# A transformer block on one core: DeltaNet's inverse doubling in eight steps, and a head's output transposes moved behind two later projections

## The chip, the cores and the metric

The kernel runs on one core of one Trainium2 chip. The metric is the device time of one execution in microseconds (us).

## What is computed

The program is one block of a diffusion transformer over 1024 tokens of width 1024 with a context of 256 tokens: layer norm and modulation, a wide input projection, a branch of differential attention (8 heads), a branch of gated DeltaNet (8 heads), a merge, and an MLP. All is in float32. The change lies in the DeltaNet branch alone. For each head and each of two directions (the sequence and its reverse) the reference computes this, chunk by chunk:

```python
a_mat = jnp.where(strict, jnp.einsum('bhnid,bhnjd->bhnij', kb, kc) * decay, 0.0)
t_mat = lax.linalg.triangular_solve(eye + a_mat, jnp.broadcast_to(eye, a_mat.shape),
                                    left_side=True, lower=True, unit_diagonal=True)
...
def step(state, xs):
    u_i, w_i, qk_i, q_i, k_i, g_i = xs
    v_new = u_i - jnp.einsum('bhid,bhde->bhie', w_i, state)
    o_i = jnp.einsum('bhid,bhde->bhie', q_i, state) + jnp.einsum('bhij,bhje->bhie', qk_i, v_new)
    state = state * g_i[..., None, None] + jnp.einsum('bhid,bhie->bhde', k_i, v_new)
    return state, o_i
...
return (rms_norm(o, norm_g) * jax.nn.silu(z)).reshape(b, length, DN_WIDTH)
```

q, k and v are projections that pass through a convolution of 7 taps and a silu; z is a projection too.

## The kernel before

The kernel works on chunks of 128 tokens: 10 chunks (2 of the context, 8 of the sequence) in each direction.

**Projections.** One head needs v, k, q and z of DeltaNet, and between them two projections ("f") of other parts of the block are filled in. `gemm_cols` (L157) computes one projection in two halves of 512 tokens, each 24 matmuls of 128x512: float32 is kept by splitting operands in a high and a low part, three matmuls for each of 8 blocks of the contraction (L167 to L169). The weights come over SP's DMA queue (L149), ScalarE makes the high part (L152), GpSimd the low part (L153). Two raw pieces and one whole projection's split pieces fit in the buffers. A projection's PSUM tile is called `pg`, of which there are two.

**A head's stages.** `dn_prep` transposes k and q, builds decay masks and, per chunk, the triangular matrix `cm` and the masked product `pm`, and inverts all diagonal 32x32 blocks on VectorE (`inverse32`, 46 operations on 104 partitions). The block inverses go to DRAM as `xd` and `yd`. `dn_double` (L587) loads them back as diagonal blocks into `cm` and `tt` (7 DMAs a direction, on SP), and builds the 128x128 inverse from 32x32 blocks by two doublings: products of 32x32, then of 64x64, with copies on VectorE (`z`, L615, L632) and ScalarE (L620, L625, L637) between. `tt` has one buffer, so direction 1's loads wait until direction 0's third product (L631) has read it. `dn_pre` makes token-major copies of v and k. `dn_chain` (L660) walks the 10 chunks of both directions: L683, L691, L679 on TensorE, ScalarE's `ws` (L686) and VectorE's `xs` (L681) and `S` (L696) depend on each other in a ring. At its end the head's output is normalized on VectorE (L722), transposed on TensorE (L726, 8 transposes into PSUM tile `po`), multiplied by the gate (L728) and written to DRAM as `odn_d` (L730).

**What sets the order.** Each engine runs one static list. A list scheduler makes it when the program is built: each operation has a rank, smaller first. The projections are written at a base rank of 6; the chain, the doubling within it and the weight loads have rank 0 (`R_CHAIN`, `R_W`), evictions of projections 0 (`R_E`), prep and pre 1 (`R_PREP`), convolutions 2 (`R_CONV`). In each turn h of the head loop the code writes pre(h), prep(h+1), double(h), chain(h), and then the projections `v`(h+1), `k`(h+2), `q`(h+2), f, f, `z`(h+1).

Of the kernel before, what the change touches and what calls it, by code (L numbers as in the profile page):

```python
# [8 lines left out]
F32 = mybir.dt.float32  # L9
# [47 lines left out]
class K:  # L57
    def __init__(self, tc, ins, out, ctx):
        self.tc, self.nc, self.i, self.out, self.ctx = tc, tc.nc, ins, out, ctx
        self.ranks = None  # L60
        self.weng = tc.nc.vector

# [94 lines left out]
    def gemm_cols(self, w, u, toks, evac, cs=slice(0, P), pool=None):  # L157
# [429 lines left out]
    def dn_double(self, h, r):  # L587
# [3 lines left out]
        tt = []  # L591
        for d in range(2):
            t = dw.tile([P, NT, 64], F32, name="tt", bufs=BK[0])
            for b, (lo, hi) in (((0, (32, 128)), (1, (64, 128)), (2, (96, 128))) if d else ((1, (0, 32)), (2, (0, 64)), (3, (0, 96)))):
                nc.gpsimd.memset(cm[d][32 * b:32 * b + 32, :, lo:hi], 0.0)
            nc.gpsimd.memset(t[96:128, :, 0:32] if d else t[0:32, :, 32:64], 0.0)
# [8 lines left out]
        for d in range(2):  # L605
            c_, t_ = cm[d], tt[d]
            pairs = ((3, 2), (1, 0)) if d else ((0, 1), (2, 3))
            sl = lambda b: slice(32 * b, 32 * b + 32)
            co = lambda b: slice(32 * (b % 2), 32 * (b % 2) + 32)
            pz = self.po.tile([P, NT, 32], F32, name="po")  # L610
            z = dw.tile([P, NT, 32], F32, name="z32", bufs=1)
            for a, b in pairs:
                for c in range(NT):
                    nc.tensor.matmul(pz[sl(b), c], lhsT=c_[sl(a), c, sl(b)], rhs=t_[sl(a), c, co(a)], start=True, stop=True)
                nc.vector.tensor_copy(out=z[sl(b)], in_=pz[sl(b)])  # L615
            py = self.po.tile([P, NT, 32], F32, name="po")
            a, b = pairs[0]
            for c in range(NT):
                nc.tensor.matmul(py[sl(b), c], lhsT=c_[sl(b), c, sl(b)], rhs=z[sl(b), c], start=True, stop=True)
            nc.scalar.copy(out=t_[sl(b), :, co(a)], in_=py[sl(b)])  # L620
            px = self.po.tile([P, NT, 32], F32, name="po")
            for a, b in pairs:
                for c in range(NT):
                    nc.tensor.matmul(px[sl(a), c], lhsT=z[sl(b), c], rhs=c_[sl(b), c, sl(b)], start=True, stop=True)
                nc.scalar.copy(out=c_[sl(a), :, sl(b)], in_=px[sl(a)])  # L625
            A, B = (slice(64, 128), slice(0, 64)) if d else (slice(0, 64), slice(64, 128))
            z6 = dw.tile([P, NT, 64], F32, name="z64", bufs=1)
            for q in range(2):
                pz = self.po.tile([P, 5, 64], F32, name="po")
                for c in range(5):  # L630
                    nc.tensor.matmul(pz[B, c], lhsT=c_[A, 5 * q + c, B], rhs=t_[A, 5 * q + c, :], start=True, stop=True)  # L631
                nc.vector.tensor_copy(out=z6[B, 5 * q:5 * q + 5], in_=pz[B])  # L632
            for q in range(2):
                px = self.po.tile([P, 5, 64], F32, name="po")
                for c in range(5):
                    nc.tensor.matmul(px[A, c], lhsT=z6[B, 5 * q + c], rhs=c_[B, 5 * q + c, B], start=True, stop=True)
                nc.scalar.copy(out=c_[A, 5 * q:5 * q + 5, B], in_=px[A])  # L637
# [22 lines left out]
    def dn_chain(self, h, r):  # L660
# [61 lines left out]
        nc.vector.tensor_tensor(out=oacc, in0=oacc, in1=so.unsqueeze(2).to_broadcast((P, NX, P)), op=ALU.mult)  # L722
        for q in range(2):
# [868 lines left out]
    def dn_phase(self):  # L1592
# [70 lines left out]
```

## Time and profile before

| | us |
|---|---|
| median of 3 runs | 3171.98 (3169.81 to 3173.66) |
| the profiled execution | 3170.53 |
| its span | 3168.8 |
| its mean granted TensorE clock | 0.949 |
| TensorE busy | 2899.6 (92%) |
| VectorE busy | 2263.7 (71%) |
| ScalarE busy | 1402.7 (44%) |
| GpSimd busy | 947.4 (30%) |

Busy time is a share of the whole span, in which stages with different limits follow one another. The DeltaNet phase lies between about 200 and 1290 us; the attention, merge and MLP behind it hold the rest. A start time below is counted from the span's start. A TensorE row's duration is the time to its modelled end, and matmuls overlap, so the distance between two starts tells what one costs.

### The profile page before, as it was taken

The numbers are of one execution on the slowest core, as the hardware profiler recorded it, in microseconds if no ns is written. First come the engines' busy times: TensorE is split into PE (matmuls) and PEld (weight loads), VectorE is DVE, ScalarE is ACT, GpSimd is POOL, SyncE is SP. The second block draws the span as 40 slices with busy tenths as digits, with TensorE's granted clock in tenths as the row PEclk, the third lists the DMA queues.
The fourth block names the chain that finished last, engine by engine and source line by source line (L and its number), as shares of the span: only waits on it lengthen the run. The fifth ranks groups of instructions, "written<-read, shape, count | busy, mean of one in ns | idle before, by whom it ended". The sixth has DMA issues, their size and how long they took to land. (4 is left out here: it accounts for less than half of the span.)

```text
span 3168.8 us, 45399 instructions
## 1 busy us (share of the span) xinstructions
PE 2899.6 (92%) x15736; PEld 2248.4 (71%) x15736; DVE 2263.7 (71%) x4202; ACT 1402.7 (44%) x3485; POOL 947.4 (30%) x959
## 2 busy tenths in 40 slices
PE   7998979989999899899999999999998999787888
PEld 4876767767778687677776777676776777566666
DVE  4678588777695873577777777644667775699999
ACT  4654344444344442355545555554456222233332
POOL 1235133342432421101000101111004533767771
PEclk9999889999998997999999999999999999898999
DMA  7531211221211212623222222316554543422222
GB/s 257 187 93 40 52 50 54 47 63 38 63 50 44 65 47 51 156 50 79 71 63 60 67 73 63 92 46 217 162 188 148 162 138 106 166 82 80 85 85 92
DMA packets 368118, 295.29 MB, mean 93 GB/s; under 512 B 88916, under 2 KB 321492, under 8 KB 366864
## 3 DMA queue, kind: packets, MB, share of 16 engines
q1 hardware_dynamic: 347920, 252.14, 27.1%
q10 hardware_dynamic: 16384, 29.54, 3.6%
q0 software_dynamic: 3584, 10.71, 0.9%
q8 instruction: 124, 2.03, 0.3%
q14 instruction: 106, 0.87, 0.1%
HBM read 212.08 MB, written 66.06 MB: 88 GB/s over the span
## 5 line engine op out<-in xcount | busy, mean ns | idle before, releaser
L153 POOL TENSOR_TENSOR wlo<-wraw,whi 128x256 fp32r<-128x256 f32 x312 | 316.6, 1020 | 1314.5 <-ACT whi L152 1146.5
L167 PE MATMUL pg<-uh,whi 128*128 128x512 f32 x1152 | 486.8, 423 | 9.4 <-ACT whi L152 6.1
L169 PE MATMUL pg<-uh,wlo 128*128 128x512 f32 x1152 | 485.3, 421 | 6.0 <-POOL wlo L153 5.9
L168 PE MATMUL pg<-ul,whi 128*128 128x512 f32 x1152 | 483.0, 419 | 0.0
L152 ACT CAST whi<-wraw 128x256 fp32r<-128x256 f32 (+1 forms) x568 | 240.9, 430 | 346.0 <-PE pg L168 95.2
L167 PEld LDWEIGHTS pg<-uh,whi 128*128 128x128 f32 x1152 | 225.7, 196 | 55.5 <-ACT whi L152 8.2
L169 PEld LDWEIGHTS pg<-uh,wlo 128*128 128x128 f32 x1152 | 225.1, 195 | 55.8 <-POOL wlo L153 11.2
L168 PEld LDWEIGHTS pg<-ul,whi 128*128 128x128 f32 x1152 | 225.2, 195 | 41.5 <-issue 4.1
L899 DVE TENSOR_REDUCE mp<-sx 128x1 f32<-128x1024 f32 x128 | 155.9, 1220 | 100.8 <-PE sx L889 100.5
L153 DVE TENSOR_TENSOR wlo<-wraw,whi 128x256 fp32r<-128x256 f32 (+1 forms) x256 | 135.4, 539 | 118.5 <-ACT whi L152 117.3
L985 PE MATMUL pa<-B,A 128*128 128x512 f32 x256 | 110.1, 431 | 69.7 <-DVE acc L1436 37.7
L1335 ACT CAST A<-araw 128x384 fp32r<-128x384 f32 (+1 forms) x144 | 66.7, 476 | 236.1 <-DVE araw L1344 107.3
L904 ACT ACTIVATE p<-sx,mx 128x1024 f32<-128x1024 f32 x128 | 143.4, 1121 | 43.4 <-DVE mx L900 39.1
L927 PEld LDWEIGHTS pat<-V,aT 128*128 128x128 f32 x1280 | 151.3, 194 | 13.2 <-ACT aT L925 10.9
L927 PE MATMUL pat<-V,aT 128*128 128x128 f32 x1280 | 159.8, 280 | 0.1
L925 ACT COPY aT<-pat 128x384 f32<-128x384 f32 (+1 forms) x192 | 78.3, 408 | 129.5 <-PE pat L924 121.3
L889 PE MATMUL sx<-kl,Q 64*128 64x512 f32 x256 | 128.3, 501 | 0.0
L924 PE MATMUL pat<-ident,p 128*128 128x128 f32 x640 | 118.8, 284 | 10.2 <-ACT aT L925 5.4
L1337 DVE TENSOR_TENSOR A<-araw,A 128x384 fp32r<-128x384 f32 (+1 forms) x144 | 123.6, 865 | 2.8 <-ACT A L1335 2.7
L888 PE MATMUL sx<-K,Q 128*128 128x512 f32 x256 | 118.9, 465 | 0.0
L985 PEld LDWEIGHTS pa<-B,A 128*128 128x128 f32 x256 | 52.0, 203 | 90.3 <-ACT A L1335 39.5
L924 PEld LDWEIGHTS pat<-ident,p 128*128 128x128 f32 x640 | 77.8, 142 | 53.6 <-ACT aT L925 19.0
(480 smaller groups left out, 7705.7 us busy)
## 6 DMA issues: line engine op xcount, KB each, us to landing
wraw<-in_w_in_dram SPq DMA_DIRECT2D x288, 128.0 KB
wraw<-in_w_in_dram SPq DMA_DIRECT2D x64, 256.0 KB
adraw<-in_w_ada_dram SPq DMA_DIRECT2D x128, 128.0 KB
uraw<-in_w_mlp_dram SPq DMA_DIRECT2D x32, 512.0 KB
braw<-in_w_mlp_dram SPq DMA_DIRECT2D x32, 512.0 KB
ff_d<-ue SPq DMA_DIRECT2D x52, 256.0 KB
araw<-ff_d SPq DMA_DIRECT2D x32, 384.0 KB
wa<-in_w_ada_dram SPq DMA_DIRECT2D x8, 1024.0 KB
```

The lines of the kernel that those rows point to most:

```text
L152: nc.scalar.copy(out=hi, in_=raw)
L153: self.weng.tensor_tensor(out=lo, in0=raw, in1=hi.bitcast(F32), op=ALU.subtract)
L167: nc.tensor.matmul(o, lhsT=hi, rhs=a, start=k == 0, stop=False)
L168: nc.tensor.matmul(o, lhsT=hi, rhs=b, start=False, stop=False)
L169: nc.tensor.matmul(o, lhsT=lo, rhs=a, start=False, stop=k == KT - 1)
L889: nc.tensor.matmul(ps, lhsT=q, rhs=low, start=False, stop=True)
L899: nc.vector.tensor_reduce(out=mp[:, m, 0:1], in_=px[m], axis=AX.X, op=ALU.max)
L904: nc.scalar.activation(out=p[:, CTX:], in_=px[m], func=AF.Exp, bias=mx[:, m:m + 1], accum_out=sp[:, 0, m:m + 1])
L924: nc.tensor.transpose(out=pt[:, c], in_=a[:, (c0 + c) * P:(c0 + c + 1) * P], identity=self.ident)
L927: nc.tensor.matmul(po, lhsT=aT[:, c], rhs=r["v"][:, c], start=c == 0, stop=c == NT - 1)
L985: nc.tensor.matmul(ps, lhsT=ah, rhs=bh, start=k == 0 and not add, stop=False, **more)
L1337: eng.tensor_tensor(out=z[1], in0=x, in1=z[0].bitcast(F32), op=ALU.subtract)
```

## The change

`dn_double` no longer issues its work. It returns eight closures, four for each direction: `first` (32x32 products, z), `second` (32x32 products into `tt` and `cm`), `third` (64x64 products, z) and `fourth` (64x64 products into `cm`). `gemm_cols` calls the next of them behind each half of a projection, as long as the list `between` holds any. The list for head h+1 is made ahead of `q`(h+2) in turn h, so that it is used up by q, f, f and z(h+1); what is left is called at the top of the next turn. For head 0, two empty closures stand ahead of the eight. The matmuls are now written at the projections' rank instead of the chain's, their copies and loads at `R_PREP`, and their PSUM tiles come from `pt` instead of `po`. Direction 0's loads are issued in its first step, direction 1's at the end of direction 0's third. The transposes of the output, the gate product and the DMA move to `dn_finish`, which is called behind the projections of v and k; for the last head, behind `fill(100)`.

```diff
@@ gemm_cols
             with self.rank(R_E):
                 evac(o, t0, n)
+            if self.between and pool is None:
+                self.between.pop(0)()
@@ dn_double
-        for d in range(2):
-            t = dw.tile([P, NT, 64], F32, name="tt", bufs=BK[0])
...
-            for b in range(4):
-                s = slice(32 * b, 32 * b + 32)
-                nc.sync.dma_start(out=cm[d][s, :, s], in_=(yd if d else xd)[d, b].rearrange("c j i -> j c i"))
-                if b != (0 if d else 3):
-                    o = 32 * (b % 2)
-                    nc.sync.dma_start(out=t[s, :, o:o + 32], in_=(xd if d else yd)[d, b].rearrange("c j i -> j c i"))
-            tt.append(t)
+        def load(d):
+            with self.rank(R_PREP):
+                t = tt[d] = dw.tile([P, NT, 64], F32, name="tt", bufs=BK[0])
...
+        def steps(d):
...
+            def first():
+                if d == 0:
+                    load(0)
+                t_, pz = tt[d], self.pt.tile([P, NT, 32], F32, name="pt")
+                z = zt[d] = dw.tile([P, NT, 32], F32, name="z32", bufs=1)
+                for a, b in pairs:
+                    for c in range(NT):
+                        nc.tensor.matmul(pz[sl(b), c], lhsT=c_[sl(a), c, sl(b)], rhs=t_[sl(a), c, co(a)], start=True, stop=True)
+                    with self.rank(R_PREP):
+                        nc.vector.tensor_copy(out=z[sl(b)], in_=pz[sl(b)])
...
+            def third():
...
+                    with self.rank(R_PREP):
+                        nc.vector.tensor_copy(out=z6[B, 5 * q:5 * q + 5], in_=pz[B])
+                if d == 0:
+                    load(1)
...
+            return [first, second, third, fourth]
+
+        return steps(0) + steps(1)
@@ dn_chain
+        r["o"] = oacc
+
+    def dn_finish(self, h, r):
+
+        nc = self.nc
+        oacc, sz = r["o"], r["z"]
         for q in range(2):
             pt = self.po.tile([P, 4, P], F32, name="po")
@@ the head loop
         proj(0, "v")
+        self.between = [lambda: None] * 2 + self.dn_double(0, R[0])
         proj(1, "k", "q")
         proj(0, "z")
         for h in range(H):
+            while self.between:
+                self.between.pop(0)()
...
             with self.rank(R_CHAIN):
-                self.dn_double(h, R[h])
                 self.dn_chain(h, R[h])
             if h == H - 1:
                 self.fill(100)
+                self.dn_finish(h, R[h])
                 self.fill_head()
-            for c in ORD:
+            for n, c in enumerate(ORD):
+                if n == 2:
+                    if h + 1 < H:
+                        self.dn_finish(h, R[h])
+                        self.between = self.dn_double(h + 1, R[h + 1])
```

The order on TensorE shows where the steps come to stand. Names are out<-in; `pg` is a projection, `tt`, `cm` and `z` are the doubling's, `pc` the chain's. This is the doubling of head 3's second direction before; it lies among the steps of the first direction's chain:

```order
L679 MATMUL pc_7569<-S_7545,kT 128x128
L531 MATMUL pt<-qT,kT 128x128 x2
L168 MATMUL pg<-ul,whi 128x512
L683 MATMUL pc_7569<-xs_7571,cm 128x128
L614 MATMUL po<-tt,cm 32x32 x10
L169 MATMUL pg<-uh,wlo 128x512
L167 MATMUL pg<-uh,whi 128x512
L168 MATMUL pg<-ul,whi 128x512
L614 MATMUL po<-tt,cm 32x32 x10
L619 MATMUL po<-z_7413,cm 32x32 x10
L169 MATMUL pg<-uh,wlo 128x512
```

The first direction had its doubling ahead of the chain, with projections between its groups. After the change the same head's doubling of both directions reads like this, from its second group on:

```order
L633 MATMUL pt<-z_6725,cm 32x32 x10
L170 MATMUL pg<-uh,wlo 128x512
L168 MATMUL pg<-uh,whi 128x512
L169 MATMUL pg<-ul,whi 128x512
L639 MATMUL pt<-cm,z_6725 32x32 x10
L170 MATMUL pg<-uh,wlo 128x512
L624 MATMUL pt<-tt,cm 32x32 x10
L649 MATMUL pt<-tt,cm 64x64 x10
L639 MATMUL pt<-cm,z_6725 32x32 x10
L660 MATMUL pt<-cm,z_6877 64x64 x10
L624 MATMUL pt<-tt,cm 32x32 x20
L633 MATMUL pt<-z_6999,cm 32x32 x10
```

The second direction (from the `x20`) follows the first at once, and nothing of the chain or of the projections stands between.

The second place is the start of head 3's chain on TensorE. Before:

```order
L683 MATMUL pc_7501<-vtok,cm 128x128
L470 MATMUL pt<-ugh,r_gt 128x512
L470 MATMUL pt<-ugl,r_gt 128x512
L473 MATMUL pt<-r_neg_130,r_id 128x512
L691 MATMUL pc_7501<-ws_7503,ktok 128x128
L169 MATMUL pg<-uh,wlo 128x512
L167 MATMUL pg<-uh,whi 128x512
L168 MATMUL pg<-ul,whi 128x512
L679 MATMUL pc_7515<-S_7506,kT 128x128
L169 MATMUL pg<-uh,wlo 128x512
```

After (L712, L720 and L708 are the chain's L683, L691 and L679; L678 and L685 belong to `dn_pre`, L492 to `dn_prep`):

```order
L712 MATMUL pc_7508<-vtok,cm 128x128
L678 MATMUL pt<-ident,vT 128x128 x3
L685 MATMUL pt<-ident,kT 128x128 x8
L720 MATMUL pc_7501<-ws_7503,ktok 128x128
L720 MATMUL pc_7508<-ws_7510,ktok 128x128
L685 MATMUL pt<-ident,kT 128x128 x2
L492 MATMUL pt<-ident,kT 128x128
L708 MATMUL pc_7515<-S_7506,kT 128x128
L492 MATMUL pt<-ident,kT 128x128
L708 MATMUL pc_7525<-S_7513,kT 128x128
```

Both directions now step together, and transposes of the same and the next head stand where matmuls of the projections stood. Of a head's 288 projection matmuls, 254 stand in one stretch behind the chain and prep, and `dn_finish`'s transposes stand behind the first 73 of these.

## Rows read from the trace of the kernel before

**Rows 1.** The page's head, and its busy time by engine.

```profile
span 3168.8 us, 45399 instructions
...
PE 2899.6 (92%) x15736; PEld 2248.4 (71%) x15736; DVE 2263.7 (71%) x4202; ACT 1402.7 (44%) x3485; POOL 947.4 (30%) x959
```

**Rows 2.** Busy time by stretch: length, engines' busy (count), granted clock, DMA share, GB/s.

```profile
443.25:573.60 130.35, 119.70 (x831) 95.89 (x830) 106.92 (x240) 66.97 (x191) 54.67 (x64) 0.96 0.20 53
682.30:834.20 151.90, 138.17 (x884) 111.30 (x884) 108.52 (x249) 69.05 (x195) 56.70 (x69) 0.90 0.20 54
1093.00:1204.30 111.30, 104.86 (x774) 86.07 (x774) 81.29 (x191) 47.80 (x128) 28.53 (x36) 0.98 0.21 55
1204.30:1289.40 85.10, 83.67 (x589) 67.25 (x589) 26.42 (x83) 27.86 (x85) 9.06 (x13) 0.78 0.17 44
```

**Rows 3.** TensorE's waits, 200 to 1350: us in total, times, longest.

```profile
PE po L726 <- DVE oacc L722: 25.9, 7, 10.9
...
PE po L614 <- DMA tt<-yd: 4.1, 2, 2.3
```

**Rows 4.** TensorE's timeline, pieces: start, duration, instruction, [idle before].

```profile
323.82 0.81 PE L614 MATMUL po<-tt,cm 32*32 32x32 f32 x20
...
1093.04 0.81 PE L614 MATMUL po<-tt,cm 32*32 32x32 f32 x20
...
1201.81 0.39 PE L168 MATMUL pg<-ul,whi 128*128 128x512 f32 x1
1202.04 0.40 PE L169 MATMUL pg<-uh,wlo 128*128 128x512 f32 x1
1204.27 0.79 PE L614 MATMUL po<-tt,cm 32*32 32x32 f32 x20 [1.83 <-DMA tt<-yd]
...
1206.77 1.27 PE L619 MATMUL po<-z,cm 32*32 32x32 f32 x20
...
1224.55 0.79 PE L683 MATMUL pc<-vtok,cm 128*128 128x128 f32 x2
...
1289.43 1.09 PE L726 MATMUL po<-ident,oacc 128*128 128x128 f32 x8 [1.30 <-DVE oacc L722]
```

**Rows 5.** Busy time by stretch, in two doublings, columns as in rows 2.

```profile
573.00:593.00 20.00, 20.00 (x218) 16.55 (x218) 10.94 (x29) 6.65 (x15) 8.21 (x13) 1.00 0.10 16
...
1205.00:1225.00 20.00, 20.00 (x145) 14.74 (x143) 1.97 (x4) 2.72 (x7) 1.82 (x3) 0.51 0.17 36
```

**Rows 6.** SP's queue, waits between 200 and 1300.

```profile
SPq L602 <- PE po L631: 101.1, 8, 15.1
```

**Rows 7.** VectorE's timeline, first operation and last copy of head 0's inverse.

```profile
274.70 0.47 DVE L568 TENSOR_TENSOR slY<-slX,slL 104x2 f32<-104x2 f32 x1
...
317.63 1.11 DVE L548 COPY slY<-slX 104x1024 f32<-104x1024 f32 x1
```

**Rows 8.** VectorE by line, 330 to 1200: busy us, mean ns | idle before.

```profile
L443 DVE SCALAR_TENSOR_TENSOR kT<-cvraw,taps,kT 128x772 f32<-128x772 f32 (+1 forms) x72 | 64.1, 891 | 0.0
L568 DVE TENSOR_TENSOR slY<-slX,slL 104x2 f32<-104x2 f32 (+14 forms) x105 | 52.1, 496 | 0.8
...
L585 DVE TENSOR_REDUCE slX<-slY 104x64 f32<-104x256 f32 (+3 forms) x28 | 22.8, 814 | 0.4
...
L632 DVE COPY z<-po 64x320 f32<-64x320 f32 x28 | 13.7, 489 | 44.8 <-PE po L631 44.7
```

**Rows 9.** ScalarE by line, 330 to 1200, columns as in rows 8.

```profile
L686 ACT ACTIVATE ws<-pc,bdl 128x128 f32<-128x128 f32 x126 | 46.2, 368 | 78.2 <-PE pc L683 76.8
...
L625 ACT COPY cm<-po 32x320 f32<-32x320 f32 x28 | 11.7, 416 | 37.1 <-PE po L624 37.1
```

**Rows 10.** TensorE's timeline in head 2's chain, one chain step apart.

```profile
614.27 0.39 PE L691 MATMUL pc<-ws,ktok 128*128 128x128 f32 x2
...
617.53 0.49 PE L691 MATMUL pc<-ws,ktok 128*128 128x128 f32 x2
```

More of the change, by code (lines that the diff above doesn't have):

```diff
@@ L61, in __init__ @@
         self.weng = tc.nc.vector
+        self.between = []
     def pool(self, name, bufs=1, **kw):
@@ L590, in dn_double @@
         cm, xd, yd = r["cm"], r["xd"], r["yd"]
-        tt = []
-        for d in range(2):
-            t = dw.tile([P, NT, 64], F32, name="tt", bufs=BK[0])
-            for b, (lo, hi) in (((0, (32, 128)), (1, (64, 128)), (2, (96, 128))) if d else ((1, (0, 32)), (2, (0, 64)), (3, (0, 96)))):
-                nc.gpsimd.memset(cm[d][32 * b:32 * b + 32, :, lo:hi], 0.0)
-            nc.gpsimd.memset(t[96:128, :, 0:32] if d else t[0:32, :, 32:64], 0.0)
-            for b in range(4):
-                s = slice(32 * b, 32 * b + 32)
-                nc.sync.dma_start(out=cm[d][s, :, s], in_=(yd if d else xd)[d, b].rearrange("c j i -> j c i"))
-                if b != (0 if d else 3):
-                    o = 32 * (b % 2)
-                    nc.sync.dma_start(out=t[s, :, o:o + 32], in_=(xd if d else yd)[d, b].rearrange("c j i -> j c i"))
-            tt.append(t)
@@ L605, in dn_double @@
-        for d in range(2):
-            c_, t_ = cm[d], tt[d]
-            pairs = ((3, 2), (1, 0)) if d else ((0, 1), (2, 3))
[L608 to L612, printed above, removed]
-                for c in range(NT):
[L614 to L637, printed above, removed]
@@ new lines, in dn_double @@
+        sl = lambda b: slice(32 * b, 32 * b + 32)
+        co = lambda b: slice(32 * (b % 2), 32 * (b % 2) + 32)
+        tt, zt = {}, {}
+        def load(d):
+            with self.rank(R_PREP):
+                t = tt[d] = dw.tile([P, NT, 64], F32, name="tt", bufs=BK[0])
+                for b, (lo, hi) in (((0, (32, 128)), (1, (64, 128)), (2, (96, 128))) if d else ((1, (0, 32)), (2, (0, 64)), (3, (0, 96)))):
+                    nc.gpsimd.memset(cm[d][32 * b:32 * b + 32, :, lo:hi], 0.0)
+                nc.gpsimd.memset(t[96:128, :, 0:32] if d else t[0:32, :, 32:64], 0.0)
+                for b in range(4):
+                    s = sl(b)
+                    nc.sync.dma_start(out=cm[d][s, :, s], in_=(yd if d else xd)[d, b].rearrange("c j i -> j c i"))
+                    if b != (0 if d else 3):
+                        o = 32 * (b % 2)
+                        nc.sync.dma_start(out=t[s, :, o:o + 32], in_=(xd if d else yd)[d, b].rearrange("c j i -> j c i"))
@@ new lines, in steps, with second, fourth @@
+        def steps(d):
+            c_ = cm[d]
+            pairs = ((3, 2), (1, 0)) if d else ((0, 1), (2, 3))
+            A, B = (slice(64, 128), slice(0, 64)) if d else (slice(0, 64), slice(64, 128))
+            def first():
[8 more added lines that the diff above has]
+                        nc.vector.tensor_copy(out=z[sl(b)], in_=pz[sl(b)])
+            def second():
+                t_, z = tt[d], zt[d]
+                py = self.pt.tile([P, NT, 32], F32, name="pt")
+                a, b = pairs[0]
+                for c in range(NT):
+                    nc.tensor.matmul(py[sl(b), c], lhsT=c_[sl(b), c, sl(b)], rhs=z[sl(b), c], start=True, stop=True)
+                with self.rank(R_PREP):
+                    nc.scalar.copy(out=t_[sl(b), :, co(a)], in_=py[sl(b)])
+                px = self.pt.tile([P, NT, 32], F32, name="pt")
+                for a, b in pairs:
+                    for c in range(NT):
+                        nc.tensor.matmul(px[sl(a), c], lhsT=z[sl(b), c], rhs=c_[sl(b), c, sl(b)], start=True, stop=True)
+                    with self.rank(R_PREP):
+                        nc.scalar.copy(out=c_[sl(a), :, sl(b)], in_=px[sl(a)])
+            def third():
+                t_ = tt[d]
+                z6 = zt[d] = dw.tile([P, NT, 64], F32, name="z64", bufs=1)
+                for q in range(2):
+                    pz = self.pt.tile([P, 5, 64], F32, name="pt")
+                    for c in range(5):
+                        nc.tensor.matmul(pz[B, c], lhsT=c_[A, 5 * q + c, B], rhs=t_[A, 5 * q + c, :], start=True, stop=True)
+                    with self.rank(R_PREP):
+                        nc.vector.tensor_copy(out=z6[B, 5 * q:5 * q + 5], in_=pz[B])
+                if d == 0:
+                    load(1)
+            def fourth():
+                z6 = zt[d]
+                for q in range(2):
+                    px = self.pt.tile([P, 5, 64], F32, name="pt")
+                    for c in range(5):
+                        nc.tensor.matmul(px[A, c], lhsT=z6[B, 5 * q + c], rhs=c_[B, 5 * q + c, B], start=True, stop=True)
+                    with self.rank(R_PREP):
+                        nc.scalar.copy(out=c_[A, 5 * q:5 * q + 5, B], in_=px[A])
+            return [first, second, third, fourth]
```

## The prediction

> **What bounds the kernel now.** The page comes first, for the whole: span 3168.8 us, TensorE busy 92% [rows 1]. The change touches only the DeltaNet phase, from about 320 to 1290 us, so the table by head comes next, one stretch from the start of one head's doubling to the start of the next head's [rows 2]. In it TensorE is busy for 91 to 94% of most stretches, and no other engine comes near: the period of a head is TensorE's work, plus what it idles, plus what the lower clock takes. The six periods from the first doubling at 323.82 to the seventh at 1093.04 last 769.2 us, 128.2 us each; the eighth doubling follows 111.2 us later, the last chain starts 20.3 us after that, and the last output transposes 64.9 us after that [rows 4]. The list of waits names what TensorE idles for: the biggest entry is the transposes of L726 waiting for VectorE's scaled output, 25.9 us in 7 times (some 3.4 us a head); the doubling's own waits are small, 4.1 us for its loads, and of similar size for its copies [rows 3]. Last, the clock: a doubling with many matmuls of the projections in it runs at 1.00, one without falls to 0.51, half clock, with VectorE nearly idle and TensorE busy all the time [rows 5].
>
> **What the change does to the order.** The diff reads as if each of the eight steps would stand between two halves of a projection. The order that is built says otherwise. In every head the 140 matmuls of the doubling stand in one block with 8 matmuls of the projections among them, right ahead of the chain. The chain of that head and the next head's prep then hold only some 30 matmuls of the projections, none in the first half, where before 1 to 4 stood between nearly any two chain steps. The other 254 stand in a third block, with the eight output transposes 73 matmuls into it. So a period after is a sum of three stretches: P = C (doubling) + A (chain and next prep) + B (projections).
>
> **B, the projections.** Two neighbouring projection matmuls start 0.235 us apart (1201.81 and 1202.04) [rows 4]: 254 x 0.235 = 59.7 us. The moved transposes take 1.09 us [rows 4] and should wait for nothing, since 73 matmuls (17 us) cover VectorE's scaling; if that cover were too short, the old 3.4 us would be back. B = 61 us. VectorE has nearly as much to do: about 21 convolution steps at 0.89 us (19), the inverse at (52.1 + 33.7 + 37.0 + 40.2 + 22.8 + 22.8) / 7 = 29.8 us, of which [rows 8] has the first and last of the six lines, finish and copies 5, loads 5: 59 us. Neither hides the other's growth, so B is 60 to 64, and I take 61.5.
>
> **C, the doubling.** A group of 20 small matmuls takes 0.79 us at full clock and 1.27 at half [rows 4], so the 280 instructions cost 10.5 us of TensorE at full clock; with the 8 projection matmuls 12.4. But in one block they are a string of dependences: direction 0 up to its third step is five groups of 0.4 to 0.8 us and four copies of 0.42 (ScalarE) to 0.49 us (VectorE) [rows 8, 9], at least 4.5 us; before, with projections between, head 6 took 12.9 us (1093.04 to about 1105.9). Its last blocks are loaded by issues that stand among weight loads on SP's queue, so I place the third step's end at 9.6. Only then is the single buffer `tt` free, and direction 1's loads are issued: the same wait is there before, 101.1 us in 8 times on SP [rows 6], hidden under the chain's steps; now the next matmul is its own consumer. A load trip is about half of the 5.1 us from the last copy of the inverse to the first doubling matmul (318.74 to 323.82) [rows 4, 7], say 2.5. Then direction 1: groups 3.5, copies 1.8, hand-offs 1.1, together 6.4. C = 18.5 at full clock. Half the clock adds 3.9 for the groups on that string, 22.4. Here the stretch looks most like head 7's doubling, VectorE and the projections nearly out of it, which ran at 0.51, so I take 21.5 (18 to 23).
>
> **The clock and the skill.** In the row of 1205 to 1225 TensorE is busy without a gap and still gets 0.51 [rows 5]; what came before it was one idle gap of 1.83 us [rows 4]. The Trainium skill, "TensorE: Matmul & The Clock Gate", section "HAM oscillation — how this bites in real kernels", blames idle gaps of the engine for falling back to the low clock. By that rule a doubling that follows 181 dense matmuls and has only short gaps would keep full speed, C would be 18.5 and the whole come out as in the no-change rival; the row speaks against it, since the engine there did not idle and the clock did not come back.
>
> **A, chain and prep.** Both directions of a chain step take 3.3 to 3.4 us alone (614.27 to 617.53, L691 to L691) [rows 10]: ten give 34. The first step waits for ScalarE's token copies, some 4 us more. Prep's VectorE work is in the same stretch, 12 convolutions of 0.9 and some 21 small operations, 16 us in sum [rows 8]; all of it on the string gives 54, none 38. ScalarE alone has 20 + 20 scalings at 0.37 (14.6) [rows 9] and with its other work of that stretch some 44. I take 51 (45 to 58). TensorE has only 38 us to do there: 13 us of idling per head that before was filled with projections. **That is the main loss.**
>
> **What goes away.** The wait of L726 (3.4 a head), the doubling's waits (about 1.5 a head), and the weaving of the inverse with convolutions and chain: head 0's ran from 274.70 to the copy at 317.63 [rows 7], 43 us for 29.8 of its own. All of this is in the sum already, since A, B and C are built up from work.
>
> **The sum.** P = 21.5 + 51 + 61.5 = 134, against 128.2. The start: inverse 0 without interruption ends at 274.7 + 29.8, the copy 1.1 and the load trip 5.1 follow, with 1.3 for small things: first doubling at 312 instead of 323.8. Six periods, then the seventh head's, which has no k and q to project (192 instead of 288 matmuls): 29 + 50 + 38, with hand-offs 120. The last doubling with 71 projection matmuls in it takes 28 to its chain, the last chain to the transposes 48 (ten steps 34, first step 4, norm and scale 10; before 64.9, slowed by the projections between). The last transposes are then at 312 + 6P + 120 + 28 + 48 = 508 + 6P = 1312, against 1289.4: 22.6 later. From there the order has 91 projection matmuls ahead of the first attention score where before had 121: 30 x 0.235 = 7, I count 6 back. Net +16.6 on the profiled 3170.5: 3187. The median of the runs is 1.5 us above the profiled run, so I say 3188, +0.5%. The break-even is P = 131.2.
>
> **Rivals.**
> 1. *Faster: the three stretches at their floors.* The clock stays full in the doubling (C 18.5), prep's VectorE work falls into the chain's gaps (A 45), B is TensorE's bare 61: P = 124.5, last transposes at 1255, -34 - 6 = -40, so 3130. For it: TensorE's own work of a head at full clock is about 111, and the idle of L726 goes. Against: it needs all three floors at once; partial ones (P = 128) give -19.
> 2. *Much slower: the low clock reaches into the chain.* C 22.4, and the chain begins at half clock with no projection to bring the engine back; matmuls on the string of a step get half as fast, A 58, and VectorE sets B at 64: P about 144.5, last transposes at 1375, +86 - 6 = +80, so about 3250. For it: the last head, with fewer projections, ran at 0.78 before [rows 2]. It decides once P passes 140.
> 3. *No change:* P between 130 and 132.3; the filled idle of L726 and the shorter inverse are worth just what the unfilled chain costs. About 3169.
> That the change does not do what its words say (steps spread between halves) is not a rival but the forecast's ground: the order shows it.
>
> **How the numbers follow.** A microsecond in P is six in the time, so P's uncertainty of about 6 either way is 40 us. Chances: forecast (P 132.3 to 140) 0.43, much slower 0.15, no change 0.13, faster 0.29. The range 3130 to 3255 leaves out about a tenth at each end (P under 124.5, over 145); the forecast's own range is 3176 to 3224. A measurement of this kernel tells about 0.2%, 6.3 us, from no change: faster 0.29, same 0.13, slower 0.58.
>
> **What would show it.** Right: after each doubling TensorE is busy well under 80% for some 50 us with no waits on L761, while 250 projection matmuls run without a gap elsewhere; new waits on the doubling's loads, direction 1's above all, some 2.5 us a head; a granted clock near 0.5 in C; periods of 132 to 140. Wrong: periods under 130, or chain steps of 3.4 us in spite of prep, or the doubling at 1.00. If the chain's first half is slow because of VectorE's convolutions, the waits on xs and S will show it.

## The result and the profile after

The changed kernel takes 3293.61 us (median of 4 runs, 3286.65 to 3294.8) against 3172.82 us in the same job; the ratio is 1.0372, 95% interval 1.0349 to 1.0396. It is 3.7% slower, about 120 us. The forecast was 3188, with a range that ended at 3255: the sign was right, the size was a seventh of what came.

The head of the page of the changed kernel, beside [rows 1]: the span grew by 116 us, TensorE's busy time by only 46.

```profile
span 3284.9 us, 45350 instructions
...
PE 2945.3 (90%) x15736; PEld 2308.8 (70%) x15736; DVE 2264.7 (69%) x4202; ACT 1406.3 (43%) x3489; POOL 897.3 (27%) x959
```

The table by head of the changed kernel, cut like [rows 2] from one doubling's start to the next (stretch and length, then busy time of PE, PEld, DVE, ACT and POOL with counts, granted clock, DMA share, GB/s):

```profile
607.70:751.92 144.22, 131.23 (x844) 109.45 (x843) 98.57 (x215) 61.14 (x172) 40.45 (x57) 0.88 0.19 48
751.92:895.95 144.03, 129.81 (x844) 107.86 (x843) 98.89 (x215) 60.70 (x172) 41.20 (x57) 0.89 0.19 49
...
1188.33:1325.22 136.89, 112.73 (x757) 92.49 (x756) 77.93 (x191) 51.84 (x156) 28.93 (x35) 0.88 0.18 46
1325.22:1404.06 78.84, 66.50 (x568) 53.05 (x569) 24.27 (x83) 30.88 (x97) 8.44 (x13) 0.94 0.20 51
```

Every full period is now 144 to 147 us, where before they were 109 to 152 and 128.2 in the mean. The six full periods as one stretch, in the same columns, before and after:

```profile
323.82:1093.04 769.22, 703.12 (x4816) 567.42 (x4815) 569.88 (x1240) 347.83 (x994) 261.68 (x305) 0.92 0.20 52
```

```profile
316.60:1188.33 871.73, 782.54 (x5055) 652.49 (x5055) 594.63 (x1290) 364.97 (x1033) 237.99 (x331) 0.88 0.19 49
```

Of the 102.5 us more, TensorE idles for 23 and counts as busy for 79. An estimate from these two rows of what the lower clock takes: 0.12 x 871.73 = 105 us against 0.08 x 769.22 = 62, so some 40 more at most. The rest of the busy time was not taken apart; a matmul that stands alone counts to its modelled end (0.39 us for one whose neighbours in a dense row start 0.23 apart), so a TensorE that counts as busy is not always one that has enough to do.

The starts that the sum in the prediction used, from TensorE's timeline of the changed kernel (first doubling, seventh, eighth, and the last head's transposes; L624 is the first product of a doubling, L761 the transposes):

```profile
316.60 1.24 PE L624 MATMUL pt<-tt,cm 32*32 32x32 f32 x20 [15.05 <-DMA tt<-yd]
...
1188.33 0.81 PE L624 MATMUL pt<-tt,cm 32*32 32x32 f32 x20
...
1325.22 0.92 PE L624 MATMUL pt<-tt,cm 32*32 32x32 f32 x20 [1.64 <-DMA tt<-yd]
...
1404.06 1.97 PE L761 MATMUL po<-ident,oacc 128*128 128x128 f32 x8 [8.94 <-DVE oacc L751]
```

Six periods of (1188.33 - 316.60) / 6 = 145.3 us. The stages of the period from 751.92, in the same columns: the doubling; chain and prep; and the projections, cut at the inverse's first operation and at the copy behind its last.

```profile
751.92:777.95 26.03, 22.71 (x294) 19.50 (x293) 3.90 (x8) 4.93 (x12) 2.37 (x5) 0.64 0.20 39
777.95:825.40 47.45, 44.26 (x289) 39.33 (x289) 35.24 (x112) 36.15 (x113) 11.57 (x14) 0.91 0.02 7
...
825.40:852.81 27.41, 25.55 (x115) 20.25 (x114) 27.31 (x48) 9.84 (x27) 13.14 (x18) 1.00 0.37 96
852.81:885.76 32.95, 30.61 (x130) 23.79 (x128) 31.40 (x49) 8.57 (x18) 11.01 (x15) 1.00 0.20 57
885.76:895.95 10.19, 6.68 (x23) 4.99 (x23) 1.03 (x1) 1.22 (x3) 3.11 (x5) 0.83 0.42 116
```

In the first row VectorE is busy for 3.9 of 26 us, and it works on the inverse later (second of the three stretches of the projections), with nothing of the chain beside it: the stages follow one another.

Where the projections are in the meantime, TensorE's, VectorE's and ScalarE's timelines of the changed kernel show (start, duration, instruction, idle before). First TensorE in the doubling, up to the first projection matmul behind it (L168):

```profile
756.60 0.81 PE L624 MATMUL pt<-tt,cm 32*32 32x32 f32 x20
758.00 0.79 PE L649 MATMUL pt<-tt,cm 64*64 64x64 f32 x10 [0.59 <-DVE z L626]
759.38 1.32 PE L649 MATMUL pt<-tt,cm 64*64 64x64 f32 x10 [0.59 <-DVE z L651]
760.63 1.27 PE L639 MATMUL pt<-cm,z 32*32 32x32 f32 x20
...
775.86 1.11 PE L678 MATMUL pt<-ident,vT 128*128 128x128 f32 x4
...
779.65 0.84 PE L678 MATMUL pt<-ident,vT 128*128 128x128 f32 x3
...
802.75 0.48 PE L168 MATMUL pg<-uh,whi 128*128 128x512 f32 x1
```

Then the convolution of the next v, and the copy that empties a projection tile:

```profile
781.65 0.98 ACT L444 ACTIVATE vT<-cvraw,taps 128x772 f32<-128x772 f32 x1
```

```profile
782.72 1.02 DVE L446 SCALAR_TENSOR_TENSOR vT<-cvraw,taps,vT 128x772 f32<-128x772 f32 x1 [7.95 <-ACT vT L444]
```

```profile
801.72 0.58 ACT L435 COPY cvraw<-pg 128x512 f32<-128x512 f32 x1
```

From 756.6 to 802.75 TensorE runs not one projection matmul. Read with the program's buffers (one for v, two raw ones, two `pg` tiles), the rows make a chain: `dn_pre`'s last reading of the old v (L678, 779.65) frees v's one buffer; the convolution of the next v starts at 781.65 and ends on VectorE at 801.5; that frees a raw buffer, into which q is copied at 801.72; that frees a `pg` tile; the next projection matmul starts at 802.75. And `dn_pre` itself stood behind the doubling.

Of TensorE's waits between 200 and 1500 (us in total, times, longest), the transposes' is where it was in [rows 3], 25.9 us then; those for weights (6.1 us before) and for the gate's buffer (1.8 us) grew.

```profile
PE pg L168 <- ACT whi L153: 31.0, 8, 5.5
PE po L761 <- DVE oacc L751: 27.3, 8, 8.9
PE pt L624 <- DMA tt<-yd: 17.3, 3, 15.1
PE pg L168 <- ACT sz L461: 11.1, 6, 5.7
```

### The profile page after: what moved, and what is told of

It is laid out like the page before. It is cut to its first block, busy times and chain, and to the rows that moved or that the text cites. A ratio compares the mean times of both kernels' runs of the same rounds, so it can differ in the third digit from the quotient of the medians.

```text
span 3284.9 us, 45350 instructions
## 1 busy us (share of the span) xinstructions
PE 2945.3 (90%) x15736; PEld 2308.8 (70%) x15736; DVE 2264.7 (69%) x4202; ACT 1406.3 (43%) x3489; POOL 897.3 (27%) x959
## 5 line engine op out<-in xcount | busy, mean ns | idle before, releaser
L154 POOL TENSOR_TENSOR wlo<-wraw,whi 128x256 fp32r<-128x256 f32 x312 | 269.2, 867 | 1219.6 <-ACT whi L153 1105.3
L168 PE MATMUL pg<-uh,whi 128*128 128x512 f32 x1152 | 478.3, 415 | 52.0 <-ACT whi L153 31.0
L169 PE MATMUL pg<-ul,whi 128*128 128x512 f32 x1152 | 473.2, 411 | 0.0
L170 PE MATMUL pg<-uh,wlo 128*128 128x512 f32 x1152 | 470.4, 408 | 1.2 <-POOL wlo L154 0.9
L168 PEld LDWEIGHTS pg<-uh,whi 128*128 128x128 f32 x1152 | 223.3, 194 | 109.2 <-ACT whi L153 34.5
L626 DVE COPY z<-pt 32x320 f32<-32x320 f32 x32 | 15.6, 487 | 183.2 <-PE pt L624 183.2
L1372 DVE TENSOR_TENSOR A<-araw,A 128x384 fp32r<-128x384 f32 (+1 forms) x144 | 130.4, 912 | 2.4 <-ACT A L1370 2.3
L446 DVE SCALAR_TENSOR_TENSOR vT<-cvraw,taps,vT 128x772 f32<-128x772 f32 (+1 forms) x96 | 91.9, 958 | 57.4 <-ACT vT L444 56.7
```

Source lines behind the costliest of these rows:

```text
L154: self.weng.tensor_tensor(out=lo, in0=raw, in1=hi.bitcast(F32), op=ALU.subtract)
L1372: eng.tensor_tensor(out=z[1], in0=x, in1=z[0].bitcast(F32), op=ALU.subtract)
```

## The experiments

Ratios are against the kernel before, in the same job on the same chip, each with its 95% interval. Medians of the kernel before differ by some us from job to job.

**e1: the moved transposes alone.**

```diff
 (the kernel before)
+        r["o"] = oacc
+
+    def dn_finish(self, h, r):
...
+                if n == 2:
+                    if h + 1 < H:
+                        self.dn_finish(h, R[h])
```

> The kernel before with only the output transposes moved behind the projections of v and k (the doubling stays where it was, in PSUM tile po). Theory 1 (the loss of the changed kernel comes from the doubling's steps alone, through their PSUM tiles): the order keeps some 60 projection matmuls in each chain, so no loss; of the 25.9 us that L726 waited, up to 15 to 25 may be won: 3145 to 3172. Theory 2 (moving the transposes blocks something too, since the gate's buffer and its DMA are freed later and SP's weight loads stand behind that DMA): 3180 to 3220.

Measured 3178.61, ratio 1.0036 (1.0010 to 1.0061), some 11 us slower. Neither figure: the move wins nothing, and costs a little. In its trace the transposes wait for VectorE longer than the 25.9 us before:

```profile
PE po L732 <- DVE oacc L722: 32.6, 8, 10.9
```

VectorE's scaling does not come later. In the first seven heads it starts 18 to 27 us behind the chain's last matmul (18 to 25 before), and the projections of v and k that now stand ahead of the transposes do not always cover that.

**e2: the steps alone.** The changed kernel with the transposes written at the chain's end again.

```diff
-                        self.dn_finish(h, R[h])
                         self.between = self.dn_double(h + 1, R[h + 1])
```

> The changed kernel with the output transposes back at the chain's end; the eight steps stay. Theory 1: the whole loss is the steps', so 3275 to 3300, periods of 144 to 146 us, granted clock near 0.64 in the doubling. Theory 2: half of the loss goes, 3220 to 3260.

Measured 3291.22, 1.0396 (1.0355 to 1.0437): theory 1. All of the loss comes with the steps.

**e3: the steps with `po` for their PSUM tiles.**

```diff
-                t_, pz = tt[d], self.pt.tile([P, NT, 32], F32, name="pt")
+                t_, pz = tt[d], self.po.tile([P, NT, 32], F32, name="po")
 (and the same in the four other tiles of the doubling)
```

> The changed kernel, with the doubling's PSUM tiles taken from po again instead of pt; nothing else. Theory 1: the steps starve TensorE because the next dn_pre and its reading of v stand behind the doubling in the rotation of the two pt tiles: v's buffer comes free late, the next v convolution frees the raw buffer late, q's halves stay in both projection tiles, and no projection can run in the doubling and in the chain's first half. With po the order has 7 to 30 projection matmuls in a doubling and 60 in a chain, and the time falls to 3130 to 3185. Theory 3 (the loss lies in the steps' place, behind an inverse that comes late, and in the half clock of small matmuls; the pool is a side issue): still 3240 to 3300.

Measured 3204.21, 1.0116 (1.0066 to 1.0167). Outside the stated window by 19 us, but some 80 of the 120 us are gone with the name of a PSUM pool. A period of its trace, from doubling to doubling, clock 0.97 instead of 0.88:

```profile
722.23:855.70 133.47, 122.19 (x842) 98.09 (x841) 97.25 (x218) 58.52 (x170) 53.11 (x56) 0.97 0.20 52
```

**e4: `dn_pre` ahead of the steps, pool `pt` kept.**

```diff
                         self.dn_finish(h, R[h])
+                        with self.rank(R_PREP):
+                            self.dn_pre(h + 1, R[h + 1])
                         self.between = self.dn_double(h + 1, R[h + 1])
```

> The changed kernel, doubling still in pt, but the next head's dn_pre is written ahead of the eight steps instead of behind them, so its transposes come first in the rotation of pt. Theory 1: v's buffer is free before the doubling, the doubling gets 50 to 60 projection matmuls in it and around the chain's start, and half or more of the loss goes: 3170 to 3240. Theory 3: no change, 3280 to 3300.

Measured 3318.59, 1.0470 (1.0422 to 1.0519): slower still, so theory 1 in its narrow form (it is `dn_pre` behind the doubling that starves the projections) falls. Its trace has the period from 627.30 to 781.66:

```profile
627.30:781.66 154.36, 132.19 (x844) 105.32 (x845) 98.76 (x215) 59.56 (x170) 48.93 (x56) 0.88 0.18 46
```

Projections now run in the doubling. But the next `dn_prep` still runs behind it (on TensorE from 665.9 to 707.4), the inverse behind that (729.5 to 770.9), and then the next doubling: the same string, longer. A part of the loss is of another kind, though. TensorE now waits 67.7 us for the gate's one buffer, which comes free behind the moved transposes; in the changed kernel that wait was 11.1 us:

```profile
PE pg L168 <- ACT sz L461: 67.7, 6, 16.9
```

If these 57 us more were gone one for one (an estimate), e4 would stand near 3262, still above the 3240 of theory 1, but no longer above the changed kernel.

**e5 and e6: a longer inverse, in both kernels.** The last copy of the inverse is done nine times.

```diff
-            nc.vector.tensor_copy(out=Y[:NB], in_=X[:NB].rearrange("p a b -> p b a"))
+            for _ in range(9):
+                nc.vector.tensor_copy(out=Y[:NB], in_=X[:NB].rearrange("p a b -> p b a"))
```

> The changed kernel with the last copy of each inverse (1.03 us on VectorE) done nine times instead of once: 8.2 us more per head between the inverse and the doubling's loads. Theory 4 (the changed kernel's period is a closed string: prep, inverse, doubling, and only then the next head's prep, since the doubling's pt tiles stand ahead of the next dn_pre and dn_prep): every microsecond counts, 7 to 8 x 8.2, so 3345 to 3365. Theory 3 (the period is TensorE's work at a low clock, with small matmuls in a block): most of the delay is hidden, 3290 to 3315.

> The kernel before with the same nine copies. Theory 4: there the next head's prep does not wait for the doubling, the string is open and has slack, so less than half of 66 us is seen: 3170 to 3200. Theory 3: the same as in the changed kernel, 0 to 25 more.

Measured: the changed kernel 3326.8, 1.0506 (1.0445 to 1.0566), which is 1.3 points over its ratio without them, about 42 us of the 66 (each ratio is known to 0.2 to 0.6 points); the kernel before 3219.74, 1.0168 (1.0104 to 1.0231), about 53 of 66. None of the four stated windows holds. The traces say the same with less spread: from the first doubling to the seventh a period takes 149.7 us in e5 (320.66 to 1218.81), 4.4 more than without the copies, and 134.7 us in e6 (338.94 to 1147.36), 6.5 more. Theory 4 wanted the first to pay in full and the second less than half, theory 3 wanted most of it hidden in both. Both fall in this form: the inverse's end is nearly on the path in both kernels, and the string in the changed one has some slack. In e5 TensorE's wait for the doubling's loads rose to this, from 17.3 us (the longest wait is the one ahead of the first doubling, 15.1 us without the copies):

```profile
PE pt L625 <- DMA tt<-yd: 36.7, 9, 23.2
```

**e7: the pool alone, at the old place.** The kernel before, with the doubling in `pt`.

```diff
-            pz = self.po.tile([P, NT, 32], F32, name="po")
+            pz = self.pt.tile([P, NT, 32], F32, name="pt")
 (and the same in the four other tiles)
```

> The kernel before with one change: the doubling's PSUM tiles come from pt instead of po; place, rank and finish as before. Theory 4: the pool alone does little harm, since here dn_pre and the next dn_prep stand ahead of the doubling in the rotation of pt; 3170 to 3230. Rival (two pt tiles are too few for doubling and prep at any place): 3270 or more.

Measured 3190.42, 1.0073 (1.0045 to 1.0100): as theory 4 and its successor say. Two `pt` tiles are not too few. It is the pool together with the steps' new place and rank that costs; place and rank were not tried apart from each other in `pt`.

**e8: the transposes still later**, behind v, k, q and f.

```diff
-                if n == 2:
+                if n == 4:
                     if h + 1 < H:
                         self.dn_finish(h, R[h])
```

> The kernel before with the output transposes moved still further: behind v, k, q and the first f instead of behind v and k. If the transposes' wait for VectorE's scaling (32.6 us in 8 times when moved behind v and k) is only a matter of distance, it goes and 10 to 30 us are won: 3140 to 3162. If moving them costs by what stands behind them on SP (the gate's DMA, then weight loads): 3175 to 3210.

Measured 3205.99, 1.0105 (1.0070 to 1.0140): the second. The wait for the scaling falls, to 19.1 us in 3 times, and still more distance costs more. What holds it back (the gate's buffer, SP's queue) was not separated further.

**e9: `dn_pre` and the next `dn_prep` ahead of the steps, pool `pt` kept.** This is e4 and one thing more.

```diff
+                if n == 3 and h + 1 < H:
+                    with self.rank(R_PREP):
+                        self.dn_pre(h + 1, R[h + 1])
+                        if h + 2 < H:
+                            self.dn_prep(h + 2, R[h + 2])
+                    self.between = self.dn_double(h + 1, R[h + 1])
 (and out of the top of the turn)
```

> The changed kernel, steps between the halves and in pt, finish moved, but the next head's dn_pre and the dn_prep of the head after it are written ahead of the eight steps (which begin one projection later). Theory 5 (what bunches TensorE's order is that dn_prep of head h+2 stands behind the doubling of head h+1 in the rotation of the two pt tiles; dn_pre alone, moved in e4, was not enough): the order has 40 to 75 projection matmuls in a doubling and 60 in a chain, and most of the 120 us goes: 3160 to 3230. If the steps' place or rank is what costs, whatever pt does: 3260 to 3310.

Measured 3199.2, 1.0117 (1.0072 to 1.0161): theory 5. Pool, rank and moved transposes are as in the changed kernel, and with `dn_prep` written first some 80 us come back, as many as in e3. From the third head on a doubling holds 65 projection matmuls in the trace, where it held 8. One thing more differs: the steps begin one projection later, and that shift was not tried alone. Two periods of its trace, and where its inverse and its chain start (first L712) lie: inverse from 757.72 to the copy at 804.88, chain from 742.99 to 806.9, side by side.

```profile
599.26:728.29 129.03, 122.04 (x834) 95.50 (x834) 98.43 (x216) 62.43 (x173) 40.59 (x57) 0.97 0.21 54
728.29:858.29 130.00, 123.85 (x823) 97.46 (x822) 98.24 (x216) 59.98 (x171) 37.20 (x55) 0.93 0.20 52
```

```profile
742.99 0.63 PE L712 MATMUL pc<-vtok,cm 128*128 128x128 f32 x2
```

```profile
757.72 0.16 DVE L571 TENSOR_TENSOR slY<-slX,slL 104x2 f32<-104x2 f32 x1
...
804.88 1.12 DVE L551 COPY slY<-slX 104x1024 f32<-104x1024 f32 x1
```

**e10 and e15: two of SP's waits in the projections' stretch**, each taken off SP in the changed kernel.

```diff
-        nc.sync.dma_start(out=self.odn_d[h], in_=sz)
+        nc.gpsimd.dma_start(out=self.odn_d[h], in_=sz)
```

> The changed kernel with the gate's DMA (odn_d) on GpSimd's queue instead of SP's. In the changed kernel this DMA stands on SP ahead of nine weight loads and waits there for VectorE's gate product, and TensorE then idles some 5 us a head for weights and for the eviction of z. If that is a part of the loss in the stretch of the projections: 20 to 35 us less, 3255 to 3275. If the stretch is bound by VectorE's convolutions and inverse: 3285 to 3300.

```diff
-            nc.sync.dma_start(out=xd[d].rearrange("b c j i -> (b c) j i"), in_=X[s])
+            nc.gpsimd.dma_start(out=xd[d].rearrange("b c j i -> (b c) j i"), in_=X[s])
 (and the same for yd)
```

> The changed kernel with the four writes of each head's inverse (xd, yd) on GpSimd's queue instead of SP's. If TensorE's idle for weights in the projections' stretch (31 us in 8 times) comes from the weight loads that stand behind these writes on SP: 3260 to 3275. If the wait only moves, since GpSimd's own list then holds weight splitting behind the same write, or the stretch is held by the inverse's end anyway: 3280 to 3300.

Measured 3287.36, 1.0396 (1.0352 to 1.0440), and 3289.08, 1.0395 (1.0346 to 1.0445): no gain from either. In e10 the wait for weights stayed; in e15 it went from the weights' high part, 31.0 us in the changed kernel, to the low part that GpSimd makes, behind the same write, and new waits for the doubling's loads came beside it:

```profile
PE pg L168 <- ACT whi L153: 30.4, 7, 5.4
```

```profile
PE pg L170 <- POOL wlo L154: 38.8, 10, 5.6
...
PE pt L624 <- DMA tt<-xd: 21.7, 6, 4.2
```

**e11 and e13: what is left with the steps in `po`.** e11 is e3 with the transposes at their old place; e13 is e11 with the chain's rank for the steps' matmuls, copies and loads.

```diff
-                self.between.pop(0)()
+                with self.rank(R_CHAIN):
+                    self.between.pop(0)()
 (and no R_PREP within the steps)
```

> e3 (steps in po) with the output transposes back at the chain's end, so that only the steps' place and rank differ from the kernel before. By e1 the moved transposes cost 11 us, so if the parts add up: 3185 to 3200. If the steps' place itself is free: 3165 to 3180.

> e11 (steps between the halves, in po, finish at its old place) with the steps' matmuls, copies and loads at the chain's rank again. If the rank makes the remaining 28 us: back at the kernel before, 3160 to 3180. If the place between the halves makes them: 3190 to 3205.

Measured 3197.21, 1.0111 (1.0067 to 1.0155), and 3147.55, 0.9927 (0.9900 to 0.9954). So with the steps in `po` the lower rank costs the rest and more. e13 lies below both stated windows and beats both kernels, by 0.7% against the one before. Its first doublings start close to that one's (322.3, 444.6, 577.8 and 683.2, there 323.8, 443.3, 573.6 and 682.3), and why it is a little faster was not found out. The head of its page:

```profile
span 3147.3 us, 45394 instructions
...
PE 2886.6 (92%) x15736; PEld 2241.5 (71%) x15736; DVE 2263.1 (72%) x4202; ACT 1402.7 (45%) x3483; POOL 951.7 (30%) x959
```

**e12, e14 and e16: attempts to shorten the leg to the inverse in good kernels.** e12 is the kernel before with prep's DMAs of the diagonal blocks on GpSimd's queue, e14 the kernel before with `dn_prep` written in the turn ahead, e16 is e13 with e12's edit.

```diff
-                nc.sync.dma_start(out=ld[d, b].rearrange("c j i -> j c i"), in_=cm[d][s, :, s])
+                nc.gpsimd.dma_start(out=ld[d, b].rearrange("c j i -> j c i"), in_=cm[d][s, :, s])
```

```diff
+                if n == 3 and h + 2 < H:
+                    with self.rank(R_PREP):
+                        self.dn_prep(h + 2, R[h + 2])
```

> The kernel before with prep's DMAs of the diagonal blocks (cm to DRAM and back for the inverse, ten a head) on GpSimd's queue instead of SP's, where they stand behind weight loads (in head 1 from 457.8 to 487.5). By e6 a delay of 8.2 us between prep and doubling costs 6 a head in the kernel before, so a leg that gets shorter by 4 to 8 us should win 20 to 50 us: 3120 to 3150. If GpSimd's queue is no faster or its weight splitting gets in the way: 3160 to 3200.

> The kernel before with dn_prep of head h+2 written in turn h behind v, k and q of that turn, not at the top of turn h+1; nothing else. By e6 a delay of the inverse costs the kernel before 6 of 8 us, and by e9 an earlier dn_prep lets the inverse run beside the chain. If the inverse's end is what the kernel before waits for: 3110 to 3155. If it is not (TensorE's own work of a head, 111 us at full clock, and the rest is clock): 3160 to 3200.

> e13 (steps between the halves, in po, at the chain's rank, transposes at their old place) together with e12's move of prep's DMAs to GpSimd's queue. If the two small gains add (0.7% and 0.2%): 3135 to 3150. If they overlap: 3150 to 3165.

Measured 3160.0, 0.9978 (0.9946 to 1.0009); 3175.62, 1.0011 (0.9987 to 1.0035); 3170.96, 1.0019 (0.9993 to 1.0044). None differs from the kernel before; e12 and e14 lie in their second windows, e16 above both of its own. Written earlier, `dn_prep` wins nothing in the kernel before, where no doubling stands ahead of it in its pool; in the changed kernel (e9) it won some 80 us. The gain of e13 did not survive a change of queue that costs nothing by itself; a gain of this size may hang on details of the order.

## Why the prediction was right or wrong

**What bounds the kernel, and that the steps bunch: right.** The order was read, the three stretches stood as forecast, and TensorE gets 8 projection matmuls in the doubling and none in the chain's first half. That it would idle there was wrong (see A).

**Why they bunch: missing.** The prediction took the order as given. The runs name the cause. PSUM tiles of a pool go round in the order in which the code asks for them. The steps ask for `pt` tiles in turn h; `dn_pre`(h+1) and `dn_prep`(h+2) ask in turn h+1 and so stand behind them, and can't start before the doubling of head h+1, which waits for that head's inverse. So inverse h+2 can't run beside chain h+1, as it does in e9, and v's buffer comes free late. e7 (pool without the new place and rank), e3 (place and rank without the pool) and e9 (all of it, but prep written first) all lose at most 1.2%; all together lose 3.7%. What e3 still loses goes with the steps' rank (e11 against e13). e4 shows that `dn_pre` alone was not it, with a loss of its own beside it.

**The sum, term by term.** By the spans, 3168.8 + 16.6 = 3185.4 was forecast and 3284.9 came, 99.5 more:

| term | forecast | measured | difference |
|---|---|---|---|
| first doubling starts | 312 | 316.6 | +4.6 |
| six periods | 6 x 134 | 6 x 145.3 | +67.7 |
| seventh period | 120 | 136.9 | +16.9 |
| last doubling to last transposes | 76 | 78.8 | +2.8 |
| behind them, against before | -6 | +1.5 | +7.5 |

**B is the term that failed**: 61.5 forecast, 27.41 + 32.95 + 10.19 = 70.55 measured. All six periods, cut alike, give 70.6 to 72.9 for B, 25.7 to 26.7 for C and 46.6 to 47.5 for A: of the 11.3 us that P is off, B has about 10, C adds 4.6 and A takes 3.7 away. B was costed from TensorE's 254 matmuls (59.7) with VectorE's string at 59 beside it, "60 to 64". VectorE's string is longer, and VectorE is busy for 58.7 of the 60.4 us up to the inverse's end: 27.4 us from prep's last matmul to the inverse's first operation, where some 24 were counted (with "finish and copies" among them), 33.0 for the inverse instead of 29.8 (its 46 operations sum to 30.8; a gate product and what lies between dependent ones make the rest), and 10.2 from the copy to the next doubling, where 5 were counted for the loads, since the inverse's writes, weight loads and the loads follow one another on SP. That this string holds the stretch is argued, not shown: it fits e10 and e15, where waits of TensorE were moved and nothing came of it, and e5, where 8.2 us more of it gave 4.4 a period. In the first leg SP also issues prep's ten DMAs of the diagonal blocks, with weight loads between, from 826.55 to 846.95; whether these or VectorE's convolutions set the start of the inverse was not tried in the changed kernel. TensorE idles 7.7 us in B: 1.86 at the transposes, whose "cover of 17 us" was too short for a scaling that starts 21 us behind the chain's last matmul, 1.35 for the gate's buffer, 3.86 for weights that stand on SP behind the write of the inverse, 0.63 for GpSimd.

**C: 21.5 forecast, 26.0 measured.** Half clock was taken for the string of products, 22.4 at most. The clock did fall, in the middle: a group of 20 takes 0.81 us up to 756.6 and 1.27 from 760.6, and the stretch has 0.64 (0.50 from 759.40 on). The rest is 3.3 us of idling between groups and the transposes of `dn_pre`, whose first stand ahead of the last group. So the level that the prediction read from [rows 5] was right. The wait that the sum holds for direction 1's loads, 2.5 us a head, did not come: in the whole changed kernel TensorE waits 2.5 us in 2 times for them at direction 1's first product. Between 751.92 and the first slow group the longest gaps in the rows are 0.59 us, and full speed was not kept. The Trainium skill ("TensorE: Matmul & The Clock Gate", section "HAM oscillation — how this bites in real kernels") puts the fall to the low clock down to idle gaps; these rows do not bear out what the prediction drew from that rule. Elsewhere in the trace a gap does go with half clock: behind 3.86 us without work, at 889.27, projection matmuls start 0.42 to 0.59 us apart (granted clock 0.50 from 889.20 to 892.00), and from 892.36 on 0.23 again.

```profile
885.01 0.40 PE L170 MATMUL pg<-uh,wlo 128*128 128x512 f32 x1
889.27 0.79 PE L168 MATMUL pg<-uh,whi 128*128 128x512 f32 x1 [3.86 <-ACT whi L153]
889.86 0.63 PE L169 MATMUL pg<-ul,whi 128*128 128x512 f32 x1
...
892.36 0.39 PE L169 MATMUL pg<-ul,whi 128*128 128x512 f32 x1
```

**A: 51 forecast, 47.4 measured**, inside the bounds, but not by the mechanism. The prediction called 13 us of idling a head the main loss, and "well under 80%" busy its sign; TensorE counts as busy for 44.3 of the 47.4 us and idles 3.2. The 38 us of work that were counted there became 44.3, since the first 8.75 us run at half clock, which takes up to 4.4 of them; the rest was not taken apart. The rows are the doubling from the fall of the clock on, the chain up to its return, and on to the next projection:

```profile
759.40:777.95 18.55, 16.40 (x195) 14.67 (x195) 2.43 (x5) 3.29 (x8) 0.71 (x2) 0.50 0.12 18
777.95:786.70 8.75, 7.90 (x36) 7.12 (x36) 3.37 (x7) 6.53 (x18) 0.00 (x0) 0.51 0.00 0
786.70:802.75 16.05, 13.71 (x98) 11.75 (x97) 13.77 (x32) 14.12 (x61) 5.54 (x6) 1.00 0.00 1
```

**The range** failed for a reason of its own. Its upper end was P = 145, and P came out at 145.3. But it held only P's uncertainty: 32 us of the other terms' errors, all to the same side, had no place in it. The seventh period is the largest of them: there no projection stands ahead of the transposes, which wait 5.51 us, and the 156 projection matmuls behind them took 48 us, 7 of it idle, instead of 38.

**The rivals.** "Much slower" gave 3250 by the low clock reaching into the chain. Its time was nearest, and its P of 144.5 met 145.3 by luck: A was 47.4 and not 58, B 70.6 and not 64, C 26.0 and not 22.4. Its reason was partly right: the low clock does reach into the chain, for 8.75 us, and then full clock comes back with no projection run. That VectorE sets B was named there too, at 64. "Faster" needed three floors at once; none was reached.

**The moved transposes.** "The wait of L726 goes" was wrong: 27.3 us in 8 times afterwards, 32.6 in e1.

## What to carry to other kernels

When work is written earlier in the program, ask which rotating buffers it takes and who asks for these next: it pushes all of them behind itself, and behind everything that it waits for. A stretch that looks bound by one engine with another close behind needs both strings laid end to end with their queue positions, since whichever is under-counted sets the stretch; and an error in a period that repeats is multiplied, while errors in the terms at both ends add to it.

## What the runs showed of the hardware

In the doubling of the changed kernel the granted clock fell from full to half between the rows at 756.60 (0.81 us for a group of 20 products) and 760.63 (1.27 us), with no idle gap over 0.59 us in the rows between, while TensorE counts as busy for 22.7 of 26 us of that stretch. Busy time in the profile is no sign that the clock holds. Full clock came back at about 786.70 with transposes and chain matmuls of 128x128 alone, 16 us ahead of the next projection matmul, so a return does not need a projection.
